# Normalisation after the product for a part of a projection, with a new order of loads

## The chip, the cores and the metric

The kernel runs on one core of a Trainium2 chip. The metric is the device time of one execution in microseconds. Matrix products run on TensorE (PE in the profile), elementwise work on VectorE (DVE) and ScalarE (ACT), transfers are issued by SyncE (SP) and by ScalarE.

## The reference

One layer works on a residual stream `x` of 512 tokens by 2048 features. What matters here is its beginning:

```python
mod = c_act @ w_ada[l] + b_ada[l]
shift, scale, gate = jnp.split(mod, 3, axis=-1)
h = rms_norm(x) * (1.0 + scale[:, None, :]) + shift[:, None, :]
proj = h @ w_in[l]
xr, gr, qc, kvc, kr, ga = jnp.split(proj, split_points(IN_SPLITS), axis=-1)
```

`rms_norm` multiplies each token by the reciprocal root of its mean square. `proj` has 4160 columns. Then come a recurrent branch (convolution, gates, scan), a latent attention with eight heads, both with gates, and an output product with 2048 x 2048 weights. All is float32.

## The kernel before

Features lie on the partitions and tokens run along the 512 columns of a tile. The features are cut into 16 blocks of 128 (index k). The wide projection's columns are cut into 32 output tiles of 128 (index m, in the order `MORDER`) and a narrow one of 64 for `kr`. Every float32 factor is split into a high and a low part, so that a product of one block with one output tile is three matmuls of 512 columns: high weight by high `h`, high weight by low `h`, low weight by high `h`. For weights, ScalarE copies the raw tile to `whi` and VectorE subtracts to get `wlo` (`wload`, L193); two buffers of each stand in the first phase, and three to five raw ones.

**The start.** SP's queue carries first the eight half rows of `xtok` (512 KB each), whose squares are summed by ScalarE and VectorE (`xsq`, L364), then `vec`, `m0` (the scale columns for block 0, 1 MB) and pieces of the modulation matrix. From the sums comes `rx`, the factor per token (L411 to L418). The heads of `xtok` are multiplied by `rx`, transposed on TensorE (L436), and scaled to block 0 of `h`. The scale column for block 0 is a product of 16 small matmuls into `mr_ps`, copied to a row and turned into a column by `m0_ps`. `junk` matmuls (`warm`) fill TensorE at three places. Block 0 of the first eight output tiles is multiplied by exact float32 products (`wfraw`), two passes each.

**Rows.** Each shift or scale column of the other blocks is a row sum: 1 MB of `ada` is loaded, multiplied by the broadcast `cb` and summed by one VectorE instruction (`ttr`, L271). A scale row and a shift row make one `h` block (`make_h`, L453): two VectorE passes and one of ScalarE. Three buffers hold rows.

**Chunks.** The 16 blocks are multiplied in four chunks (`CHUNKS`: 2, 3, 4 and 7 blocks). Within a chunk the output tiles go by groups (`proj_group`, L522); after each chunk a tile's sum is copied (first chunk, ScalarE) or added (VectorE) to its slot `pj` (`evac`, L512). The rows for the next chunk are spread over the groups of this one (L579 to L584). The last chunk (7 blocks, `proj_last`) runs together with the recurrent branch, then attention and the output product follow.

**Order.** SP's order is that of the program text. The other engines' orders are laid out by the scheduler of the framework, from a simulated timeline; `tc.issue_after` puts an instruction behind a given one. `setup_rope` (rotary tables) and `setup_sp` (constants of the recurrence) stand in the last chunk (`SETUP`, L740 to L743).

Of the kernel before, what the change touches and what calls it, by code (L numbers as in the profile page):

```python
# [12 lines left out]
F32 = mybir.dt.float32  # L13
# [7 lines left out]
P = 128  # L21
# [4 lines left out]
CHUNKS = ((0, 2), (2, 3), (5, 4), (9, 7))  # L26
# [6 lines left out]
NF = 8  # L33
GROUP = (4, 2, 2, 1)
AHEAD = (0, 1, 0)
# [5 lines left out]
SETUP = (0, 2)  # L41
WARM = (4, 5, 2)
SQ_V = (3, 6)
# [40 lines left out]
def body(ctx, nc, tc, a):  # L84
# [49 lines left out]
    def mm_hi(out, wh, c0, xs, start):  # L134
        for i, (xh, xl) in enumerate(xs):
            mm(out, wh[:, cols(c0 + i)], xh, start and i == 0, False)
            mm(out, wh[:, cols(c0 + i)], xl, False, False)

    def mm_lo(out, wl, c0, xs, stop):
        for i, (xh, _) in enumerate(xs):  # L140
            mm(out, wl[:, cols(c0 + i)], xh, False, stop and i == len(xs) - 1)
# [51 lines left out]
    def wload(src, n):  # L193
        raw = wraw()
        DMA.dma_start(out=raw[:, :n], in_=src)
        hi, lo = wtile("whi", "whi"), wtile("wlo", "wlo")
        wlast[0] = ins_of(split(hi[:, :n], lo[:, :n], raw[:, :n]))
        return hi, lo
# [12 lines left out]
    ktab = pjt(33, F32, "ktab").rearrange("p (f i c) -> p f i c", f=2, i=NT)  # L211
# [5 lines left out]
    c4 = pjt(20, F32, "c4")[0:4]  # L217
    A.dma_start(out=c4, in_=a["c"])
    ccol = p1.tile([P, NK], F32, name="ccol")
    A.dma_start(out=ccol, in_=a["ccol"])  # L220
    id4 = p1.tile([4, 4], F32, name="id4")
    A.dma_start(out=id4, in_=a["row"][0:4, R_ID:R_ID + 4])
# [9 lines left out]
    ch, cl = (pjt(21 + i, F32R, f"c4{n}")[0:4] for i, n in enumerate("hl"))  # L232
    sel = pjt(23, F32R, "sel")[0:4].rearrange("p (q o) -> p q o", q=4)
    V.tensor_copy(out=sel, in_=id4.rearrange("p (q o) -> p q o", o=1).broadcast_to([4, 4, P]))
    tab(c4, c4, AF.Silu)
    V.tensor_copy(out=ch, in_=c4)
    tt(cl, c4, ch.bitcast(F32), ALU.subtract)

    junk = p1.tile([P, S], BF16, name="junk")
    V.memset(junk, 1.0)  # L240
    junk_ps = bank("aux", "junk_ps")

    def warm(n, after=None):
        with tc.issue_after(ins_of(after)) if after is not None else nullcontext():
            for _ in range(n):
                mm(junk_ps, junk[:, :P], junk, True, True)

    warm(WARM[0])
    cps = [bank("mm", "cb_ps") for _ in range(4)]
    for r in (ch, cl):  # L250
        for q in range(4):
            mm(cps[q], sel[:, q], r, r is ch, r is cl)
    for q in range(4):
        V.tensor_copy(out=cb[:, q], in_=cps[q])
# [4 lines left out]
    def xslot(name):  # L259
        n = xn[0]  # L260
        xn[0] += 1
        return pjt((36, 37, 34, 35)[n % 4], F32, name)
# [15 lines left out]
    def ada(j, parts=(4,)):  # L278
        t = p1.tile([P, 4, S], F32, tag="ada", name="ada", bufs=3)
        n0 = 0  # L280
        for w in parts:
            c = slice(n0, n0 + w)
            DMA.dma_start(out=t[:, c], in_=a["ada"][j][:, n0 * S:(n0 + w) * S].rearrange("p (k s) -> p k s", k=w))
            ttr(t[:, c], cb[:, c], j, n0 == 0, n0 + w == 4)
            n0 += w
            yield


    def setup_rope():
        rt = [pjt(34 + i, F32, f"rt{i}") for i in range(2)]  # L290
# [49 lines left out]
    def setup_sp():  # L340
# [3 lines left out]
        act(ab, lam, AF.Abs)  # L344
# [17 lines left out]
    sqj, sqv = (bigt(n, "sqj").rearrange("p k s -> p (k s)") for n in (15, 14))  # L362

    def xsq(i, j):  # L364
        t = bigt((2, 3, 8, 9, 10, 11, 12, 13)[2 * i + j], "xtok").rearrange("p k s -> p (k s)")
        DMA.dma_start(out=t, in_=a["xtok"][i][:, j * 1024:(j + 1) * 1024])
        s = ss8[:, j * 4 + i:j * 4 + i + 1]
        if 2 * i + j in SQ_V:
            sq = V.tensor_tensor_reduce(out=sqv, in0=t, in1=t, op0=ALU.mult, op1=ALU.add, scale=1.0, scalar=0.0,
                                        accum_out=s)  # L370
        else:
            sq = act(sqj, t, AF.Square, accum_out=s)
        if not i and not j:
            with tc.issue_after(ins_of(sq)):
                tab(ccol, ccol, AF.Silu)
        if j == 0:
            xhead.append(t[:, :KT0 * P])
        warm(WARM[1], sq)

    hh, hl, xhead = {}, {}, []  # L380
    KT0 = CHUNKS[0][1]
    NG = NF // 4
    wfs = {(k, n): bigt(4 + k * NG + n, "wfs", F32R) for k in range(1, KT0) for n in range(NG)}
    wfraw = {kn: pjt(16 + i, F32, "wfraw") for i, kn in enumerate((k, n) for k in range(KT0) for n in range(NG))}

    def wf_load(k, n):
        raw = wfraw[k, n]
        DMA.dma_start(out=raw, in_=a["winf"][k, n])
        if k:
            act(wfs[k, n][:, 0], raw, AF.Copy)  # L390

    def wf_lo(k, n):
        tt(wfs[k, n][:, 1], wfraw[k, n], wfs[k, n][:, 0].bitcast(F32), ALU.subtract)

    A.dma_start(out=ident, in_=a["row"][:, R_ID:R_ID + P])
    xps = [bank("mm", "xps") for k in range(KT0)]
    for n in range(2 * NT):
        xsq(n // 2, n % 2)
    DMA.dma_start(out=vec, in_=a["vec"])
    ts(vec[:, 16:32], vec[:, 16:32], 1.0, None, ALU.add)  # L400

    m0 = [bigt(4 + q, "m0").rearrange("p k s -> p (k s)").rearrange("p (b f) -> p b f", b=8) for q in range(2)]
    for q in range(2):
        DMA.dma_start(out=m0[q], in_=a["ada0"][:, 8 * q:8 * q + 8])
    run(ada(0, (2, 2)))
    for n in range(NG):
        wf_load(0, n)
    tab(p1.tile([P, 1], F32, name="sqrt0"), ones[:, 0:1], AF.Sqrt)


    vx, yx, tx, rx = (p1.tile([P, NT], F32, name=n) for n in ("vx", "yx", "tx", "rx"))  # L411
    tt(vx, ss8[:, 0:4], ss8[:, 4:8], ALU.add)
    ts(vx, vx, 1.0 / D, EPS, ALU.mult, ALU.add)
    V.reciprocal(out=tx, in_=vx)
    tab(yx, tx, AF.Sqrt)
    tt(tx, yx, yx, ALU.mult)
    stt(tx, tx, -0.5, vx, ALU.mult, ALU.mult)
    mark[0] = ins_of(stt(rx, tx, 1.5, yx, ALU.add, ALU.mult))  # L418

    for i in range(NT):  # L420
        if i % 2:
            ts(xhead[i], xhead[i], rx[:, i:i + 1], None, ALU.mult)
        else:
            act(xhead[i], xhead[i], AF.Copy, scale=rx[:, i:i + 1])

    mr_ps, m0_ps = bank("mm", "mr_ps"), bank("mm", "m0_ps")
    rb_ps = bank("aux", "rb_ps")

    for b in range(NK):
        i = mm(mr_ps[0:1, 0:P], ccol[:, b:b + 1], m0[b // 8][:, b % 8], b == 0, b == NK - 1)  # L430
    mrow = pjt(24, F32, "mrow")[0:1, 0:P]
    act(mrow, mr_ps[0:1, 0:P], AF.Copy)
    with tc.issue_after(ins_of(i)):
        for k in range(KT0):
            for i in range(NT):
                t = PE.transpose(xps[k][:, cols(i)], xhead[i][:, cols(k)], ident)  # L436
    with tc.issue_after(ins_of(t)):
        i = mm(m0_ps[:, 0:1], mrow, ones[0:1, 0:1], True, True)
    tt(mod[:, 16:17], m0_ps[:, 0:1], vec[:, 16:17], ALU.add)
    with tc.issue_after(ins_of(i)):  # L440
        for i in range(NT):
            t = mm(rb_ps[:, cols(i)], rx[:, i:i + 1].broadcast_to([P, P]), ident, True, True)
    warm(WARM[2], t)
    xt[0] = xps[0]
    for k in range(1, KT0):
        xt[k] = pjt(34 + k, F32, f"x{k}")
        act(xt[k], xps[k], AF.Copy)
    rb = p1.tile([P, S], F32, tag="rb", name="rb")
    act(rb, rb_ps, AF.Copy)

    h0 = []

    def make_h(k):  # L453
        if 0 < k < KT0:
            yield from ada(16 + k, (2, 2))
            yield from ada(k, (2, 2))
        x, sc, sh = xt[k], mod[:, 16 + k:17 + k], mod[:, k:k + 1]
        t = bigt(k, f"h{k}", F32R)
        hh[k], hl[k] = t[:, 0], t[:, 1]
        if k < KT0:  # L460
            xs = pjt(30 + k, F32, "xs")
            if k == 0:
                h0.append(xs)
                mark[0] = ins_of(ts(xs, x, sc, sh, ALU.mult, ALU.add))
                split(hh[k], hl[k], xs)
            else:
                act(xs, x, AF.Copy, scale=sc)
                ts(hh[k], xs, sh, None, ALU.add)
                mark[0] = ins_of(stt(hl[k], xs, sh, hh[k].bitcast(F32), ALU.add, ALU.subtract))
        else:  # L470
            stt(x, x, sc, rb, ALU.mult, ALU.mult)
            act(hh[k], x, AF.Identity, bias=sh)
            stt(hl[k], x, sh, hh[k].bitcast(F32), ALU.add, ALU.subtract)
        if not k:
            yield

    rows = [f + k for k in range(KT0, NK) for f in (16, 0)]
    tiles, loaded, summed = [], [0], [0]  # L480

    def row_load():
        j = rows[loaded[0]]
# [758 lines left out]
```

## Time and profile before

| | |
|---|---|
| time, median of three runs | 714.48 us (714.46 to 715.6) |
| span of the profiled execution | 712.3 us |
| TensorE busy | 706.0 us, 99% |
| VectorE busy | 537.5 us, 75% |
| ScalarE busy | 356.5 us, 50% |
| first projection matmul starts | 22.47 us |
| matmuls and weight loads | 3284 each |
| bytes moved | 131.60 MB, mean 185 GB/s |

The page names lines of the kernel (L124 is the helper that issues a matmul), an operation's output and inputs by tile names, and for groups the busy time and the mean duration of one. The time between instructions of one engine is put down to what released the next. The granted clock of TensorE is 1.00 nearly throughout.

### The profile page before, as it was taken

What the parts mean: (1) busy time and instruction counts of PE and PEld (TensorE: products, weight loads), DVE (VectorE), ACT (ScalarE), POOL (GpSimd) and SP (SyncE); (2) the same over time, 40 slices, a digit from 0 to 9 for tenths busy, and PEclk for the clock granted to TensorE, in tenths of its full rate; (3) what the DMA queues carried; (4) which work ended last, traced back from release to release, by engine and by line L of the source; (5) the groups of instructions that cost most, each with busy time, mean ns of one, the idle gap of its engine ahead of it and who ended that gap; (6) DMA issues with size and microseconds to landing.
All of it is one profiled execution on the core that took longest, in us unless ns stands there. A gap on an engine that the chain in (4) does not pass through costs nothing.

```text
span 712.3 us, 9598 instructions
## 1 busy us (share of the span) xinstructions
PE 706.0 (99%) x3284; PEld 579.7 (81%) x3284; DVE 537.5 (75%) x1008; ACT 356.5 (50%) x767; POOL 33.3 (5%) x50
## 2 busy tenths in 40 slices
PE   8999999999999999999999999999999999999997
PEld 4688888888888888888888898888888888788886
DVE  4857999899997989888756666659797886683332
ACT  6376222222223589885455677687766433222220
POOL 0000000000000000001002102002110000000000
PEclk9999999999999999999999999999999999999999
DMA  9998777697532422233253326323552887875320
GB/s 337 408 399 315 262 278 265 248 343 293 197 140 75 137 82 79 77 91 104 70 163 108 107 86 208 111 74 117 157 184 82 301 271 271 282 253 175 117 88 30
DMA packets 48880, 131.60 MB, mean 185 GB/s; under 512 B 5820, under 2 KB 12860, under 8 KB 45248
## 3 DMA queue, kind: packets, MB, share of 16 engines
q1 hardware_dynamic: 41472, 109.94, 44.9%
q10 hardware_dynamic: 7360, 21.06, 8.4%
q8 instruction: 26, 0.43, 0.2%
q14 instruction: 22, 0.18, 0.1%
HBM read 126.78 MB, written 4.19 MB: 184 GB/s over the span
## 4 chain that ended last, share of the span: by engine, by line
PE 95%; DMA 3%; DVE 1%; issue 0%; SPq 0%; ACT 0%; ACTq 0%; DVEq 0%
PE pp L124 48%; PE oa L124 24%; PE uwkv L124 6%; PE uwq L124 5%; PE sc L124 4%; PE op L124 2%; DMA ada<-in_ada 1%; PE tp L945 1%; DMA xtok<-in_xtok 1%; PE pk L124 1%; PE tq L857 1%; PE pi L124 1%; PE pr L124 1%; DMA ccol<-in_ccol 1%; DVE ada L273 1%; PE tqe L905 0%
## 5 line engine op out<-in xcount | busy, mean ns | idle before, releaser
L124 PE MATMUL pp<-h,whi 128*128 128x512 f32 x992 | 240.8, 390 | 0.0
L89 ACT ACTIVATE whi<-wraw 128x512 fp32r<-128x512 f32 (+4 forms) x192 | 136.5, 717 | 196.8 <-PE pp L124 100.3
L124 PEld LDWEIGHTS pp<-h,whi 128*128 128x128 f32 x992 | 185.7, 188 | 38.6 <-ACT whi L89 0.2
L117 DVE TENSOR_TENSOR wlo<-wraw,whi 128x512 fp32r<-128x512 f32 (+4 forms) x192 | 150.9, 791 | 69.7 <-ACT whi L89 34.5
L124 PE MATMUL pp<-h,wlo 128*128 128x512 f32 x496 | 126.9, 390 | 0.0
L124 PEld LDWEIGHTS pp<-h,wlo 128*128 128x128 f32 x496 | 92.9, 188 | 19.0
L124 PE MATMUL oa<-yl,whi 128*128 128x512 f32 (+1 forms) x260 | 100.9, 389 | 0.0
L124 PE MATMUL oa<-yh,whi 128*128 128x512 f32 (+1 forms) x260 | 100.1, 390 | 0.1
L117 DVE TENSOR_TENSOR pj<-pp,pj 128x512 f32<-128x512 f32 x96 | 64.7, 685 | 15.1 <-PE pp L124 14.8
L124 PE MATMUL oa<-yh,wlo 128*128 128x512 f32 (+1 forms) x260 | 71.0, 390 | 0.0
L273 DVE CUSTOM_DVE_ANT_0 ada<-ada,cb,vec 128x2048 f32<-128x2048 f32 (+1 forms) x31 | 69.5, 2242 | 1.7 <-DMA ada<-in_ada 1.7
L124 PEld LDWEIGHTS oa<-yh,whi 128*128 128x128 f32 x260 | 48.7, 188 | 10.2 <-ACT yh L89 0.5
L124 PEld LDWEIGHTS oa<-yl,whi 128*128 128x128 f32 x260 | 48.9, 188 | 9.3
L124 PEld LDWEIGHTS oa<-yh,wlo 128*128 128x128 f32 x260 | 47.8, 188 | 9.4
L124 PE MATMUL uwkv<-whi,kvt 128*128 128x512 f32 x80 | 28.4, 398 | 0.0
L228 POOL TENSOR_TENSOR hs<-hs,mhalf 128x4 f32<-128x4 f32 (+1 forms) x20 | 24.5, 1227 | 1.6
L124 PE MATMUL uwq<-whi,kvt 128*128 128x384 f32 x80 | 24.1, 344 | 0.1
L89 ACT ACTIVATE PT<-tp 128x128 f32<-128x128 f32 (+3 forms) x32 | 14.0, 438 | 19.1 <-PE tp L945 10.8
L124 PE MATMUL sc<-kT,qT 128*128 128x128 f32 (+3 forms) x96 | 23.0, 327 | 0.0
L273 DVE CUSTOM_DVE_ANT_0 ada<-ada,cbo,vec 128x1024 f32<-128x1024 f32 x16 | 20.4, 1278 | 3.1 <-DMA ada<-in_ada 3.1
L273 DVE CUSTOM_DVE_ANT_0 ada<-ada,cbo,modh 128x1024 f32<-128x1024 f32 x16 | 20.5, 1279 | 1.9 <-DMA ada<-in_ada 1.9
L101 DVE SCALAR_TENSOR_TENSOR xo<-oa,mod,xo 128x512 f32<-128x512 f32 (+1 forms) x12 | 8.2, 704 | 17.6 <-PE oa L124 17.6
(215 smaller groups left out, 888.9 us busy)
## 6 DMA issues: line engine op xcount, KB each, us to landing
ada<-in_ada SPq DMA_DIRECT2D x28, 1024.0 KB, 5.9
ada<-in_ada ACTq DMA_DIRECT2D x32, 512.0 KB, 5.2
wraw<-in_wout SPq DMA_DIRECT2D x59, 256.0 KB, 3.8
wraw<-in_win SPq DMA_DIRECT2D x22, 512.0 KB, 5.7
wraw<-in_win SPq DMA_DIRECT2D x24, 448.0 KB, 3.2
wraw<-in_win SPq DMA_DIRECT2D x16, 384.0 KB, 5.3
wraw<-in_wkv SPq DMA_DIRECT2D x24, 256.0 KB, 3.2
wraw<-in_wq SPq DMA_DIRECT2D x24, 192.0 KB, 2.5
```

The source lines that it names most:

```text
L89: return A.activation(out=out, in_=in_, func=func, **kw)
L101: return V.scalar_tensor_tensor(out=out, in0=in0, scalar=scalar, in1=in1, op0=op0, op1=op1, **kw)
L117: return V.tensor_tensor(out=o, in0=x, in1=y, op=op)
L124: return PE.matmul(out=out, lhsT=lhsT, rhs=rhs, start=start, stop=stop, **kw)
L228: G.tensor_tensor(out=out, in0=out, in1=mhalf[:, :n], op=ALU.pow)
L273: ttr_last[0] = V.tensor_tensor_reduce(out=t, in0=t, in1=cv, op0=ALU.mult, op1=ALU.add, scale=1.0, scalar=vec[:, C_BADA + j:C_BADA + j + 1 ...
L857: PE.transpose(tp[:, d * 256 + i2 * P:d * 256 + (i2 + 1) * P], kt[:, q * P:(q + 1) * P], ident)
L945: PE.transpose(tp[:, j * P:(j + 1) * P], pr[:, j * P:(j + 1) * P], ident)
```

## The change

The factor per token is the same for all blocks of features, so it can be applied to a sum. For the first `N1` = 18 output tiles and the first `KE` = 4 blocks, the product is made with `e = x * (1 + scale)`, without the factor and without the shift. These sums wait in their slots. When the tile's next chunk (blocks 4 to 8) comes, VectorE writes slot times `rb` (the factor, spread over the partitions) into the PSUM bank, and the matmuls add to it. The shift's part is a constant per output column: `b0`, a row product of the weights (`w0t`, the same weights once more, transposed, 4.5 MB) with the shift, added in the last chunk.

The other 14 output tiles take blocks 0 to 8 in one chunk with the full `h`. So there are chunks of 4 and 5 blocks, or of 9, and one of 7. The first eight tiles of each kind run as a stream, block by block, in eight banks, with weights of 4 output tiles (256 KB) at a time. Weight loads are fetched up to three ahead (`wnext`).

The order of loads is new: `m0`, `x0` and `wu` come first in SP's queue, `ccol`, `c4i` and `vec` are on ACT's; then come the scale rows 17 to 19; the squares of `xtok` follow between the streams' loads, all on ScalarE, and `root` makes `rx` and `rb` afterwards. Block 0 comes from `x` itself, without the transposes. The full `h` of blocks 0 to 3 is made later. `setup_sp` and `setup_rope` move from the last chunk into the second. Four products of block 0 are exact float32 ones instead of eight. The junk matmuls are 8 and 3 instead of 28, 16 and 2.

The core of the diff:

```diff
-CHUNKS = ((0, 2), (2, 3), (5, 4), (9, 7))
+KE, KM = 4, 9
+KRS = ((0, 4), (4, 5), (9, 7))
-NF = 8
-GROUP = (4, 2, 2, 1)
-AHEAD = (0, 1, 0)
+NS = 8
+N1 = 18
+DEPTH = 3
+PACE = 15
+GROUP = (4, 2, 1, 1)
+RS2 = {0: 10, 1: 11, 2: 12, 3: 13, 4: 15, 5: 16, 6: 17, 7: 18, 8: 19}
-SETUP = (0, 2)
-WARM = (4, 5, 2)
-SQ_V = (3, 6)
+SETUP = (2, 6)
+WARM = (8, 3)
...
+    A.dma_start(out=c4i, in_=a["c4i"])
+    A.dma_start(out=vec, in_=a["vec"])
...
+    def xsq(n):
+        i, j = n // 2, n % 2
+        t = bigt((4, 5, 7, 8, 13, 14)[n % 6], "xtok").rearrange("p k s -> p (k s)")
         DMA.dma_start(out=t, in_=a["xtok"][i][:, j * 1024:(j + 1) * 1024])
...
+    for q in range(2):
+        DMA.dma_start(out=m0[:, 8 * q:8 * q + 8], in_=a["ada0"][:, 8 * q:8 * q + 8])
+    xload(0)
+    DMA.dma_start(out=wu, in_=a["winu"])
...
+    x0b = x0t[:, 0]
+    act(x0b, xt[0], AF.Copy, scale=vec[:, 16:17])
+    warm(WARM[0])
...
     for b in range(NK):
+        if b == NK // 2:
+            spread(ch)
+        chain(lambda: mm(mr_ps[0:1, 0:P], ccol[:, b:b + 1], m0[:, b], b == 0, b == NK - 1))
+    mrow = pjt(12, F32, "mrow")[0:1, 0:P]
+    V.tensor_copy(out=mrow, in_=mr_ps[0:1, 0:P])
+    spread(cl, range(2))
+    chain(lambda: mm(m0_ps[:, 0:1], mrow, ones[0:1, 0:1], True, True))
+    spread(cl, range(2, 4))
+    warm(WARM[1])
+    xs0 = xst[:, 0]
+    mark[0] = ins_of(stt(xs0, xt[0], m0_ps[:, 0:1], x0b, ALU.mult, ALU.add))
...
+    rows = [16 + k for k in range(1, KE)] + list(range(KE)) + [f + k for k in range(KE, NK) for f in (16, 0)]
...
+            mark[0] = wlast[0] if tie is None else tie
+            if summed[0] == 3:
+                mark[0] = rxi[0]
...
+            if 16 < j < 16 + KE:
+                k = j - 16
+                early(k)
+                act(eh[k][0], xt[k], AF.Copy, scale=mod[:, j:j + 1])
+                stt(eh[k][1], xt[k], mod[:, j:j + 1], eh[k][0].bitcast(F32), ALU.mult, ALU.subtract)
+            elif j < 16:
+                make_h(j)
...
+    def preload(m, p):
+        tt(p, slot[m], rb, ALU.mult)
...
+    def group(ms, xparts, again=False):
         ps = [bank("mm", "pp") for _ in ms]
+        if again:
+            for m, p in zip(ms, ps):
+                preload(m, p)
...
     def proj_last(n, kind, parts):
...
+                if n < N1:
+                    stt(slot[m], ps, b0[:, n:n + 1], slot[m], ALU.add, ALU.add)
+                else:
+                    tt(slot[m], ps, slot[m], ALU.add)
...
+    def bias(n):
+        t = bigt(n % 3, "w0t")
+        DMA.dma_start(out=t, in_=a["w0t"][n].rearrange("p (k s) -> p k s", k=2))
+        with tc.issue_after(wlast[0]):
+            for i in range(2):
+                V.tensor_tensor_reduce(out=t[:, i], in0=t[:, i], in1=shrow, op0=ALU.mult, op1=ALU.add,
+                                       scale=1.0, scalar=0.0, accum_out=b0[:, 2 * n + i:2 * n + i + 1])
...
+    def ahead1(k, tie):
+        row_sums(min(k + 1, 3), tie)
+        if k:
+            squares(k)
+
+    stream(MORDER[:NS], range(KE), eh, ahead1)
...
+    es = [eh[k] for k in range(KE)]
+    ng = (N1 - NS) // 2
+    for g in range(ng):
+        group(MORDER[NS + 2 * g:NS + 2 * g + 2], [es])
+        squares(3 + 3 * (g + 1))
+        if nsq[0] == 8:
+            row_sums(3 + 2 * (g - 1))
+
+    def ahead2(k, tie):
+        row_sums(RS2[k], tie)
+
+    stream(MORDER[N1:N1 + NS], range(KM), late(), ahead2)
+    n0 = summed[0]
+    NB1 = 32 - N1 - NS
+    steps = [(MORDER[n:n + 1], False) for n in range(N1 + NS, 32)] + [(MORDER[n:n + 1], True) for n in range(N1)]
+    for g, (ms, again) in enumerate(steps):
+        if g == SETUP[0]:
+            with tc.issue_after(wlast[0]):
+                setup_sp()
+        if g == SETUP[1]:
+            with tc.issue_after(wlast[0]):
+                setup_rope()
+        at = 9 * min(g + 1, NB1) + 5 * max(0, g + 1 - NB1)
+        row_sums(min(len(rows), n0 + (len(rows) - n0) * at // (9 * NB1 + 5 * N1 - PACE)))
+        if again:
+            group(ms, [hs(KE, KM)], True)
+        else:
+            group(ms, [hs(0, KE), hs(KE, KM)])
...
+        if g == NB1:
+            ps, shrow = bank("mm", "sh_ps"), bigt(3, "shrow")[:, 0]
+            for i in range(KE):
+                spread_col(ps, i, mod[:, i:i + 1])
+            act(shrow, ps, AF.Copy)
...
+        if g >= NB1 and (g - NB1) % 2 == 0:
+            bias((g - NB1) // 2)
```

The prediction calls the work on the first 18 output tiles with blocks 0 to 3 the first stream (eight tiles) and the groups (ten tiles), the next eight tiles with blocks 0 to 8 the second stream, the six tiles after them the six outputs, and the return to the 18 tiles with blocks 4 to 8 the second block.

398 lines of the change are left out of this document (183 added, 215 removed).

## The prediction

> **What bounds the kernel now.** I began with the page, whose busy times say that TensorE works through almost the whole span.
>
> ```profile
> span 712.3 us, 9598 instructions
> PE 706.0 (99%) x3284; PEld 579.7 (81%) x3284; DVE 537.5 (75%) x1008; ACT 356.5 (50%) x767; POOL 33.3 (5%) x50
> ```
>
> The median of the runs is 714.48 us, so 2.2 us lie around the span; the sums below are made in the span and get 2.2 us at the end. Does this busy time hide waits? The chain of waits in order of time (start, length, what) has a long piece of projection matmuls, and the table by stretches (length, busy time and count of PE, PEld, DVE, ACT, POOL, granted clock, DMA share, GB/s) shows VectorE beside it:
>
> ```profile
> 103.15 76.16 PE pp L124 x336
> ...
> 100.00:120.00 20.00, 20.00 (x90) 16.54 (x90) 19.40 (x25) 6.43 (x8) 0.00 (x0) 1.00 0.75 277
> 140.00:160.00 20.00, 20.00 (x90) 16.57 (x89) 20.00 (x24) 5.20 (x6) 0.00 (x0) 1.00 0.79 301
> ```
>
> 76.16/336 is 0.2267 us per 128x512 matmul, with VectorE at 97 to 100% and TensorE not waiting. So TensorE bounds everything after its first projection matmul, and two things can move the time: when that matmul starts, and whether VectorE or a transfer ever comes late. The start is in the timeline:
>
> ```profile
> 1.59 8.34 PE L124 MATMUL junk_ps<-junk 128*128 128x512 bf16 x28 [1.59 <-DVE spe L350]
> 4.75 1.06 ACT L89 ACTIVATE sqj<-xtok 128x1024 f32<-128x1024 f32 x1 [0.74 <-DMA xtok<-in_xtok]
> 5.41 0.15 PEld L124 LDWEIGHTS <-junk 128*128 128x128 bf16 x1 [0.28 <-issue]
> 5.83 3.60 PEld L124 LDWEIGHTS <-junk 128*128 128x128 bf16 x17 [0.28 <-issue]
> 6.21 0.22 ACT L89 ACTIVATE ccol<-ccol 128x16 f32<-128x16 f32 x1 [0.31 <-DMA ccol<-in_ccol]
> 9.86 1.19 PE L124 MATMUL cb_ps<-c4h,sel 4*128 4x512 f32 x4
> 14.64 1.06 ACT L89 ACTIVATE sqj<-xtok 128x1024 f32<-128x1024 f32 x1 [1.44 <-DMA xtok<-in_xtok]
> 16.13 3.65 PE L124 MATMUL mr_ps<-m,ccol 128*1 128x128 f32 x32 [0.61 <-DVE vx L117]
> 19.82 0.27 ACT L89 ACTIVATE mrow<-mr_ps 1x128 f32<-1x128 f32 x1 [1.65 <-PE mr_ps L124]
> 20.74 0.38 PE L124 MATMUL m_ps<-ones,mrow 1*128 1x1 f32 x2
> 21.05 1.16 PE L124 MATMUL rb_ps<-row,rx 128*128 128x128 f32 x8
> 21.38 0.81 DVE L114 TENSOR_SCALAR xs<-xps,mod 128x512 f32<-128x512 f32 x1
> 22.47 7.03 PE L124 MATMUL pp<-xs,wfraw 128*128 128x512 f32 x16
> 29.82 5.72 PE L124 MATMUL pp<-h,wfs 128*128 128x512 f32 x24 [0.32 <-DVE h L113]
> ```
>
> ScalarE's squares begin when a piece of `xtok` lands: the first at 4.75, the eighth at 14.64. That is (14.64 - 4.75)/7 = 1.41 us for each 512 KB once the queue runs. The scale block comes behind all eight, and the first projection matmul starts at 22.47.
>
> **The start, part by part.** The change sends the scale block `m0` (two units of 512 KB) first, then `x0` and `wu` (half a unit each). By the pitch above, unit n lands at 4.75 + 1.41(n - 1): `m0` at 4.75 and 6.2, `x0` at 6.9, `wu` at 7.6. `ccol` is now ACT's first transfer. The 32 dot-product instructions (3.65/32 = 0.114 each) run in two halves of 1.83. Junk matmuls were spaced 0.42 (5.41 to 5.83) and then 3.60/17 = 0.21, so until 5.83 I count double: the first half runs from 4.75 to 7.1. Between the halves stand four `cb_ps` matmuls (1.19), whose `c4i` is ACT's second transfer; `ccol`, second before, was read at 6.21, so silu, cast and split are done near 7.3. Second half: 8.5 to 10.3. Then the row copy (0.27), the one-column matmul (0.38) and the scaling of `x0` (like L114, 0.81), with 0.05 to 0.15 from one to the next: 11.95. The before needs 22.47 - (21.38 + 0.81) = 0.28 from there to the matmul. So it starts at **12.2 instead of 22.47: -10.3 us**. Bounds: 11.4 if `c4i` lands as early as `m0`; 16.5 if TensorE stays at the slow pace (1.8 more in each half, 0.6 in the spread).
>
> The granted clock reads 1.00 in every stretch, while those junk matmuls halve their spacing at 5.83, so that column doesn't show the pace here. [...]
>
> **TensorE's content.** Before: 7.35 us from 22.47 to 29.82 for eight exact fp32 products in two passes each. After: four, 7.03/2 = 3.51, and the twelve split matmuls that take the place of the other four, 12 x 0.2267 = 2.72. The spread of `rx` (1.16) was ahead of the first product and is now inside the stream; the spread of the four shift columns adds another 1.16. The projection is otherwise the same in count; `proj_kr` has two matmuls for each block in three chunks as in four. Net **+1.2 us**.
>
> **What lies beside it.** The durations (busy, mean ns | idle before):
>
> ```profile
> L273 DVE CUSTOM_DVE_ANT_0 ada<-ada,cb,vec 128x2048 f32<-128x2048 f32 x28 | 65.7, 2345 | 0.7 <-DMA ada<-in_ada 0.7
> L117 DVE TENSOR_TENSOR pj<-pp,pj 128x512 f32<-128x512 f32 x96 | 64.7, 685 | 15.1 <-PE pp L124 14.8
> L117 DVE TENSOR_TENSOR wlo<-wraw,whi 128x512 fp32r<-128x512 f32 x92 | 62.9, 687 | 45.2 <-PE oa L124 20.5 <-ACT whi L89 19.1 <-PE pp L124 2.3
> L117 DVE TENSOR_TENSOR wlo<-wraw,whi 128x1024 fp32r<-128x1024 f32 x22 | 26.7, 1215 | 7.5 <-ACT whi L89 7.5
> L117 DVE TENSOR_TENSOR wlo<-wraw,whi 128x768 fp32r<-128x768 f32 x16 | 15.2, 949 | 4.4 <-ACT pj L89 4.4
> L273 DVE CUSTOM_DVE_ANT_0 ada<-ada,cbo,modh 128x1024 f32<-128x1024 f32 x16 | 20.5, 1279 | 1.9 <-DMA ada<-in_ada 1.9
> L101 DVE SCALAR_TENSOR_TENSOR x<-x,mod,rb 128x512 f32<-128x512 f32 x14 | 10.4, 745 | 0.1
> ```
>
> On a full queue the instructions overlap a little, so a start-to-start price is lower:
>
> ```profile
> 102.62 2.34 DVE L273 CUSTOM_DVE_ANT_0 ada<-ada,cb,vec 128x2048 f32<-128x2048 f32 x1
> 104.89 0.08 DVE L273 DVE_READ_ACCUMULATOR2_ANT mod<- 128x1 f32 x1
> 104.89 0.68 DVE L117 TENSOR_TENSOR pj<-pp,pj 128x512 f32<-128x512 f32 x1
> 105.50 0.68 DVE L117 TENSOR_TENSOR pj<-pk,pj 128x512 f32<-128x512 f32 x1
> 106.09 0.95 DVE L117 TENSOR_TENSOR wlo<-wraw,whi 128x768 fp32r<-128x768 f32 x1
> 106.96 0.74 DVE L101 SCALAR_TENSOR_TENSOR h<-x,mod,h 128x512 fp32r<-128x512 f32 x1
> 107.62 1.28 DVE L117 TENSOR_TENSOR pj<-pp,pj 128x512 f32<-128x512 f32 x2
> ```
>
> A row sum takes 2.27, an evacuation 0.60, an `h` half 0.66, and a split 0.09 less than its duration. The rotary setup, tile `rt` alone, summed over four stretches from 160 to 240 us:
>
> ```profile
> sum 80.00, DVE 9.54 ACT 0.51; mean DVE 2.39 ACT 0.13
> ```
>
> No row shows a split of 640 columns (0.82 between 512 and 768; 0.73 on a full queue), a 512-column row product (half of 1279 plus a start: 0.75; 0.67) or an addition that writes PSUM (`preload`; 0.685 from the evacuation that reads it; 0.60).
>
> *First stream* (12.2 to 34.7). Scale row 17 is complete with unit 7, at 13.2. VectorE must first write `cb` and the low half of `e0` (about 2 us from 11.95), then sum the row and make `e1`: 17.1 to 17.9. TensorE has 3.51 + 2.72 us of block 0 and asks for `e1` at 18.4. Rows 18 and 19 land at unit 10.5 (18.1) and 15 (24.5), are ready near 21.8 and 28.2, and are asked for at 23.8 and 29.3. Margins of 0.5 to 2 us; I charge 0.5.
>
> *Groups and second stream* (34.7 to 111). The squares end with unit 26, near 40; `rx` can follow well before TensorE reaches block 0 of the second stream at 62. From 40 to 62 VectorE has three 1024-splits (3.4), six row sums (13.6) and five `h` (6.6): 23.6 for 22 us. The second stream asks 18 x 0.60 + 10 x 2.27 + 5 x 1.32 = 40 of 49 us. Tiles are now 12 matmuls (2.7 us) long instead of 18, with two buffers; a row sum ahead of a split still fits into the 2.7 + 1.8 us until its low half is wanted. Nothing charged, bound 3.7 (the same 22 us at full durations, 25.7).
>
> *Second block* (18 outputs of 15 matmuls, 61.2 + 1.16 = 62.4 us). VectorE: 18 x (0.73 + 0.60) + 18 x 0.67 + 7 x 2.27 + 4 x 1.32 + 9.54 = 66.8, so 4.4 us too much; at full durations 74.5, so 12.1. The last three outputs carry no row sum, the six outputs before (36.7 us for 27 us of VectorE) leave room for a lead of one tile, and the products for `b0` may slip into the last phase, which no longer has the rotary setup. I charge 2.0 of the 4.4. Below nothing no stage can go, since the pace is TensorE's own.
>
> The last phase exchanges an addition for one with a scalar (0.685 to 0.745), hidden under 21 matmuls of 0.2267; 4.5 MB of `w0t` and the second pass over x spread over the second block (18.5 MB in 62 us, about 300 GB/s against rates above 400 in the start). ScalarE, at 50%, takes 18 evacuations more.
>
> **Sum.** 712.3 - 10.3 + 1.2 + 0.5 + 2.0 = 705.7; with 2.2: **707.9, say 708 us**.
>
> **Rivals.**
> A, the forecast: 705.5 to 711.
> B, all VectorE work fits: 708 - 2.5 = 705.5, down to 704.5 with the early start. For it: stretches at 100% without a wait.
> C, slower: VectorE bounds the second block. Its place is the queue between row sums, rotary setup and the splits that TensorE waits for; it decides once the lead of one tile (15 matmuls, 3.4 us) is used up. Full durations instead of overlapped ones, and the overhang of the groups: 703.2 + 12.1 + 3.7 + 2.2 = 721 us; half of it is 713. For it: the sum of 66.8 against 62.4. Against it: the full stretches above.
> D, the slow pace until the stream: start at 16.5, 4.3 later: 712.
> E, the scale rows come late. The rates in the start decide:
>
> ```profile
> 10.00:15.00 5.00, 5.00 (x23) 2.71 (x24) 4.05 (x9) 2.81 (x7) 0.00 (x0) 1.00 1.02 413
> 25.00:30.00 5.00, 4.68 (x12) 1.92 (x11) 4.57 (x8) 1.98 (x3) 0.00 (x0) 1.00 1.06 412
> ```
>
> My pitch of 1.41 us for each 512 KB is 372 GB/s, below these 412, but part of it is the wait for the queue's first piece, and a load on ACT's queue shares it. If each of the three rows lands 1 us past its margin, 708 + 3 = 711. [...]
> F, the change doesn't do what it says: `m0` first but `c4i` or `vec`, both on ACT's queue, gate the chain near 22. Against it: the rows at 6.21 show a small ACT load landing within 5 us beside a full queue. Then nothing is won at the start: 712.3 + 1.2 + 2.5 + 2.2 = 718.
>
> **How the numbers follow.** A 0.50, B 0.14, D 0.10, E 0.10, C 0.13, F 0.03. From no change 0.2% (1.4 us: 713.1 to 715.9) can be told. C up to half its price and the high ends of D and E reach into that band (0.07 together); the rest of C and F lie above it: faster 0.81, same 0.07, slower 0.12. The range takes A, B, D, E and the low part of C: 704 to 714.
>
> **What would show it.** First `pp` matmul at 12.2, not 16; no `pp` matmul waiting on `e1` to `e3`; the stretch of `winc` tiles with VectorE near 100% and TensorE idle no more than 2 us. Wrong if `whi`, `wlo` or a DVE write of `pp` releases TensorE for more than 5 us in sum, or if the junk spacing stays at 0.42 into the dot products.

## The result, and the profile after

The changed kernel takes **705.83 us** (median; 705.49 to 706.34), the kernel before beside it on the same chip 714.47 us (713.68 to 715.6). The ratio is **0.988, with a 95% interval of 0.9866 to 0.9894**: faster by 1.2%. The forecast was 708.0 us with a range of 704 to 714, so the sign and the range hold and the size is 2.2 us short of what came. The profiled execution took 705.81 us, with 704.0 us of span, against 712.3 us of span before: 8.3 us less.

The page's head and its line of busy times, for the changed kernel:

```profile
span 704.0 us, 9647 instructions
PE 697.4 (99%) x3252; PEld 576.4 (82%) x3253; DVE 523.3 (74%) x1010; ACT 376.0 (53%) x812; POOL 34.9 (5%) x50
```

The shares are nearly those of before. TensorE still works through the whole span, so the difference has to be sought at the places where it does not. The timeline of the changed kernel (start, length, engine, what; in brackets the idle time before it and what ended that) has the start, one row spread over the columns, and the two later places where TensorE waited:

```profile
0.71 0.41 ACTq L226 DMA_DIRECT2D ccol<-in_ccol  x1
5.21 0.21 ACT L92 ACTIVATE ccol<-ccol 128x16 f32<-128x16 f32 x1 [1.76 <-DMA ccol<-in_ccol]
5.47 1.91 PE L127 MATMUL mr_ps<-m,ccol 128*1 128x128 f32 x16 [0.29 <-ACT ccol L92]
7.31 1.21 PE L127 MATMUL cb_ps<-c4h,sel 4*128 4x512 f32 x4
8.45 1.91 PE L127 MATMUL mr_ps<-m,ccol 128*1 128x128 f32 x16
9.63 1.36 DVE L120 TENSOR_TENSOR wlo<-wraw,whi 128x512 fp32r<-128x512 f32 x2 [1.55 <-ACT whi L92]
10.91 0.27 DVE L400 COPY mrow<-mr_ps 1x128 f32<-1x128 f32 x1
...
12.78 3.60 PE L127 MATMUL pp<-xs,wu 128*128 128x512 f32 x8
...
15.81 2.41 PE L127 MATMUL pp<-e,whi 128*128 128x512 f32 x8
17.34 0.75 DVE L104 SCALAR_TENSOR_TENSOR e<-x,mod,e 128x512 fp32r<-128x512 f32 x1 [0.79 <-ACT e L92]
18.97 1.98 PE L127 MATMUL pp<-e,whi 128*128 128x512 f32 x8
...
52.74 1.05 PE L127 MATMUL rb_ps<-row,rx 128*128 128x128 f32 x8
53.55 1.64 PE L127 MATMUL pp<-e,whi 128*128 128x512 f32 x6
...
135.50 0.77 PEld L127 LDWEIGHTS pp<-h,wlo 128*128 128x128 f32 x4 [0.47 <-DVE wlo L120]
...
214.52 0.49 DVE L120 TENSOR_TENSOR ktab<-rt,row 128x128 f32<-128x128 f32 x2
215.10 0.72 ACT L92 ACTIVATE h<-x,mod 128x512 fp32r<-128x512 f32 x1 [1.61 <-DVE ktab L120]
215.73 0.58 ACT L92 ACTIVATE pj<-pp 128x512 f32<-128x512 f32 x1
216.36 3.49 PE L127 MATMUL pp<-h,whi 128*128 128x512 f32 x14 [0.51 <-ACT pj L92]
```

The first projection matmul starts at 12.78 instead of 22.47: **9.7 us earlier**. From there to the end of the span the kernel before took 712.3 - 22.47 = 689.8 us and this one takes 704.0 - 12.78 = 691.2: **1.4 us more**. The two make the 8.3 us.

The table by stretches (length; busy time and count of PE, PEld, DVE, ACT, POOL; granted clock, DMA share, GB/s), for the first stream, the second block and the stretch behind it:

```profile
12.00:35.00 23.00, 22.84 (x94) 17.47 (x95) 15.31 (x20) 12.70 (x22) 0.00 (x0) 1.00 1.02 399
...
148.00:214.00 66.00, 66.00 (x293) 54.67 (x292) 62.28 (x134) 28.93 (x45) 0.00 (x0) 1.00 0.79 291
214.00:330.00 116.00, 115.49 (x520) 95.51 (x519) 100.21 (x151) 84.94 (x127) 4.98 (x6) 1.00 0.31 98
```

The second row holds the second block. TensorE is busy for 66.00 of 66 us there, and VectorE for 62.28: close to full, with 3.7 us left. The groups of VectorE's instructions (mean ns behind the busy time) price the three operations that had no row before:

```profile
L120 DVE TENSOR_TENSOR wlo<-wraw,whi 128x640 fp32r<-128x640 f32 x24 | 19.7, 820 | 1.8 <-ACT whi L92 1.1 <-PE pp L127 0.6
...
L120 DVE TENSOR_TENSOR pp<-pj,rb 128x512 f32<-128x512 f32 x18 | 12.4, 694 | 0.0
...
L584 DVE CUSTOM_DVE_ANT_0 w0t<-w0t,shrow 128x512 f32<-128x512 f32 x18 | 11.7, 685 | 0.4 <-DMA w0t<-in_w0t 0.4
```

### The profile page after: what moved, and what is told of

Same layout as the page of the kernel before. It is cut to its first block, busy times and chain, and to the rows that moved or that the text cites. A ratio compares the mean times of both kernels' runs of the same rounds, so it can differ in the third digit from the quotient of the medians.

```text
span 704.0 us, 9647 instructions
## 1 busy us (share of the span) xinstructions
PE 697.4 (99%) x3252; PEld 576.4 (82%) x3253; DVE 523.3 (74%) x1010; ACT 376.0 (53%) x812; POOL 34.9 (5%) x50
## 4 chain that ended last, share of the span: by engine, by line
PE 95%; DMA 2%; DVE 1%; ACT 1%; issue 1%; SPq 0%; DVEq 0%; ACTq 0%
PE pp L127 47%; PE oa L127 25%; PE uwkv L127 6%; PE uwq L127 5%; PE sc L127 4%; PE op L127 2%; PE tp L1001 1%; DMA ada<-in_ada 1%; PE pk L127 1%; PE tq L913 1%; PE pi L127 1%; PE pr L127 1%; DMA ccol<-in_ccol 1%; DMA wraw<-in_winsa 1%; PE tqe L961 0%
## 5 line engine op out<-in xcount | busy, mean ns | idle before, releaser
L92 ACT ACTIVATE whi<-wraw 128x512 fp32r<-128x512 f32 (+4 forms) x214 | 142.3, 670 | 177.3 <-PE pp L127 72.2
L127 PE MATMUL pp<-h,whi 128*128 128x512 f32 x880 | 215.6, 390 | 0.5 <-ACT pj L92 0.5
L120 DVE TENSOR_TENSOR wlo<-wraw,whi 128x512 fp32r<-128x512 f32 (+4 forms) x214 | 156.2, 735 | 77.6 <-ACT whi L92 39.0
L127 PEld LDWEIGHTS pp<-h,whi 128*128 128x128 f32 x880 | 164.6, 188 | 34.9 <-ACT pj L92 0.9
L127 PE MATMUL pp<-h,wlo 128*128 128x512 f32 x440 | 114.8, 390 | 0.0
L127 PEld LDWEIGHTS pp<-h,wlo 128*128 128x128 f32 x440 | 82.2, 188 | 17.0 <-DVE wlo L120 0.5
L275 DVE CUSTOM_DVE_ANT_0 ada<-ada,cb,vec 128x2048 f32<-128x2048 f32 x31 | 72.7, 2348 | 3.2 <-DMA ada<-in_ada 3.2
L92 ACT ACTIVATE pj<-pp 128x512 f32<-128x512 f32 x50 | 29.4, 599 | 26.9 <-PE pp L127 26.6
L127 PE MATMUL pp<-e,whi 128*128 128x512 f32 x136 | 34.5, 393 | 0.0
L127 PEld LDWEIGHTS pp<-e,whi 128*128 128x128 f32 x136 | 25.5, 188 | 5.7 <-issue 0.5
```

What stands on the lines that cost most here:

```text
L92: return A.activation(out=out, in_=in_, func=func, **kw)
L120: return V.tensor_tensor(out=o, in0=x, in1=y, op=op)
L127: return PE.matmul(out=out, lhsT=lhsT, rhs=rhs, start=start, stop=stop, **kw)
L275: ttr_last[0] = V.tensor_tensor_reduce(out=t, in0=t, in1=cv, op0=ALU.mult, op1=ALU.add, scale=1.0, scalar=vec[:, C_BADA + j:C_BADA + j + 1 ...
```

## The experiments

Each edit below also changes the order of other instructions on the engines, since that order is worked out for the whole program. A small difference between two kernels can come from this alone (the run with the row copy first shows a wait of 0.8 us that came so), and is read from the trace rather than from the time.

### The pieces of x ahead of the scale block

The question is whether the place in the queue is what brought the 9.7 us. Six pieces of x (3 MB) are loaded ahead of `m0`, and the squares use them later as before:

```diff
+    for n in range(6):
+        xtok_load(n)
     for q in range(2):
         DMA.dma_start(out=m0[:, 8 * q:8 * q + 8], ...)
```

> Six of the eight xtok pieces (3 MB) are loaded ahead of m0 in SP's queue; their squares stay where they were in the program. Theory (the gain is the earlier first product, and that is the place of m0 in the queue): m0 lands six pitches of 1.41 us later, 8.5 us; its second half at 14.7 plus 1.9 us of dot products, and from the second half's start to the first pp matmul 4.3 us as in the changed kernel: first pp matmul near 20.6 instead of 12.8, time 705.8 + 7.8 = 713 to 714 us, back at the time of before. Rival (the gain lies in the new chunks and in VectorE's relief, the start being hidden by other work): 706 to 708.

Measured: **720.22 us** (717.42 to 722.03), ratio 1.0081 (1.0054 to 1.0108), span 718.7. The whole gain is gone and 6 us more. From its timeline and its waits (what waited for what: us in total, times, longest; the first two lines are TensorE's, the last is VectorE's from 35 to 162 us):

```profile
13.28 3.57 PE L127 MATMUL mr_ps<-m,ccol 128*1 128x128 f32 x16 [8.09 <-DMA m<-in_ada]
...
21.90 2.31 PE L127 MATMUL pp<-xs,wu 128*128 128x512 f32 x5
```

```profile
PE pp L127 <- DVE wlo L120: 2.2, 3, 1.1
PE pk L127 <- DVE wkhl L120: 1.8, 1, 1.8
...
DVE ada L275 <- DMA ada<-in_ada: 11.7, 7, 2.5
```

The dot products wait 8.1 us for `m0`, and the first half of them takes 3.57 us instead of 1.91: after the wait TensorE runs slowly. The first `pp` matmul comes at 21.90, 9.1 us later. So the order of the queue is worth the gain of the start, nearly to the microsecond. The theory had named 20.6 us for this matmul and a time of 713 to 714: the span grew by 14.7, 5.6 more than the start. By the starts of TensorE's matmuls, 5.1 us went to waits on `wlo` and `wkhl`, splits on VectorE, while the 1.1 us of waits of the changed kernel (at 135 and 215 us) are not in this run: 4.0 us net. VectorE's line of the same view, for the changed kernel, gives the reason:

```profile
DVE ada L275 <- DMA ada<-in_ada: 3.2, 4, 1.6
```

Where a row sum stood at the head of VectorE's list and its scale row had not landed, the splits behind it stood too (rows of such a place, at 117 us, are in the next run): 11.7 us of such waits instead of 3.2. The last 1.6 us stand behind the longest of TensorE's waits for a split, in the timeline and in the table by stretches:

```profile
160.00 4.15 PE L127 MATMUL pk<-h,wkhl 128*128 128x512 f32 x10 [1.84 <-DVE wkhl L120]
```

```profile
160.30:164.10 3.80, 3.80 (x11) 2.93 (x10) 2.26 (x9) 0.00 (x0) 0.00 (x0) 0.55 0.28 84
```

Eight matmuls there stand 0.427 us apart, from start to start, instead of 0.227, which makes the 1.6 us, and the granted clock is 0.55.

### The scale block first, the pieces of x ahead of the scale rows

The second half of "scale rows first": the same six loads, behind the first weight tiles and ahead of the first scale row.

```diff
     def ahead1(k, tie):
+        if not k:
+            for n in range(6):
+                xtok_load(n)
         row_sums(min(k + 1, 3), tie)
```

> The same six xtok pieces are loaded behind the first three weight pieces and ahead of x1 and the first scale row; m0 keeps its place. Theory (the margins of the scale rows are about 2 us or less, so their place in the queue carries the gain as well): row 17 lands near 21.7 instead of 13.2, e1 is ready near 25 while TensorE asks for it at 19.0; one wait of 5 to 6.5 us in the first stream, none at e2 and e3, time 711 to 712.5. Rival (the rows have slack, or the loads run faster than my pitch): 706 to 707.5.

Measured: **718.13 us** (717.18 to 718.26), ratio 1.0051 (1.0035 to 1.0068), span 716.3. From its timeline:

```profile
25.40 5.38 PE L127 MATMUL pp<-e,whi 128*128 128x512 f32 x12 [6.17 <-ACT e L92]
...
117.06 2.35 DVE L275 CUSTOM_DVE_ANT_0 ada<-ada,cb,vec 128x2048 f32<-128x2048 f32 x1 [2.98 <-DMA ada<-in_ada]
...
119.34 1.29 DVE L120 TENSOR_TENSOR wlo<-wraw,whi 128x512 fp32r<-128x512 f32 x2
120.08 0.19 PEld L127 LDWEIGHTS pp<-h,wlo 128*128 128x128 f32 x1 [2.59 <-DVE wlo L120]
```

and its first stretch in the table by stretches:

```profile
12.00:35.00 23.00, 16.67 (x55) 11.66 (x56) 12.54 (x16) 11.28 (x20) 0.00 (x0) 0.85 0.91 358
```

The start is that of the changed kernel (12.81), and the wait is where the theory put it: 6.2 us on `e1`. But it cost more than its length. The twelve matmuls behind it take 5.38 us; they stand 0.427 us apart, from start to start, instead of 0.227, so 2.5 us come on top, and the granted clock of the stretch falls to 0.85. Then late scale rows come back at 117: VectorE waits 2.98 us for one, the splits behind it start at 119.34, and TensorE stands still until 120.08. Its waits for splits sum to 2.7 us on `wlo` and 0.5 on `wkhl`, 4.4 by the starts of its matmuls. Counted up by these starts, 6.3 + 2.5 + 4.4, less the 1.1 us of the changed kernel's waits that are not in this run, is 12.1 of the 12.3 us by which the span grew. The theory had the wait right and neither of its two consequences.

Slow matmuls, 0.427 against 0.227 us, came here behind a wait of 6.2 us. A wait need not be that long, though: in the run before, one of 1.8 us was followed by eight matmuls at 0.427 us. Why that one was, and the 2.2 us wait at 120 us in this run was not, stays open.

### No junk matmuls at the start

Rival D has TensorE at the slow pace until the stream. This run takes away the eight junk matmuls ahead of the dot products.

```diff
-WARM = (8, 3)
+WARM = (0, 3)
```

> The eight junk matmuls at the start are left out; the three later ones stay. [...] Rival (the pace has become full by 5.5 us whatever ran before, or the waits in the chain swallow it): first pp matmul within 0.5 us of 12.8, time 705.5 to 706.5.

Measured: **707.09 us** (706.9 to 710.22), ratio 0.9911 (0.9888 to 0.9934), span 705.1. From its timeline:

```profile
5.36 3.29 PE L127 MATMUL mr_ps<-m,ccol 128*1 128x128 f32 x16 [5.36 <-ACT ccol L92]
...
9.70 1.91 PE L127 MATMUL mr_ps<-m,ccol 128*1 128x128 f32 x16
...
13.55 1.88 PE L127 MATMUL pp<-xs,wu 128*128 128x512 f32 x4
```

Without them the first half of the dot products takes 3.29 us, 1.38 more, and the second half runs at full pace. The first `pp` matmul comes 0.77 us later, less than the 1.38, because the changed kernel's row copy waited for VectorE anyway (below). So the slow pace is real (3.29 us for 1.91) and lasts until about 8.1 us here (an estimate: at 0.114 us for a dot product at full pace and twice that at the slow one, the 1.38 us are twelve slow ones), and the eight junk matmuls are worth 0.8 us beside this profile of the changed kernel (0.45 beside its repeat, further below, where the first `pp` matmul starts at 13.10), not the 4.3 of rival D. The rival's figures did not come: 13.55 is 0.77 us from 12.8, not within 0.5, and 707.09 lies above its 705.5 to 706.5.

### More work for VectorE in the second block

This asks how far the second block is from rival C, in which VectorE bounds it. Eighteen more row products of 512 columns go behind those for `b0`, two for each `w0t` tile; their sums go to columns that nobody reads. A second kernel has nine of them (the first of each pair).

```diff
+                V.tensor_tensor_reduce(out=t[:, i], in0=t[:, i], in1=shrow, ...,
+                                       accum_out=bx[:, i:i + 1])
```

> Each of the 18 row products for b0 is followed by one more of the same size into an unused column: 18 x 0.69 = 12.4 us more of VectorE in the second block, nothing else. Theory (VectorE is within some 4 us of bounding the second block: 62.3 us busy in the 66 us from 148 to 214): 12.4 - 3.7 = 8.7 us too much, of which the last phase may take a little: 711 to 715. Rival (single small operations fill gaps and the surplus is put off into the last phase, where nothing waits): 706 to 708.

> Nine extra row products of 512 columns on VectorE in the second block (6.2 us at 0.69 each), half of what the run with eighteen had; the output is as before, the extra sums are not used. Theory (the second block has about 4 us of slack on VectorE, the 12.4 us of eighteen products cost 8.4): 2 us, 708 (ratio 0.991), with VectorE at 65 of 66 us from 148 to 214 us. Rival (VectorE is in series with TensorE at some places of the block, each product costs its share): 4.2 us, 710 (0.9938). Second rival (slack is larger, and the cost of the eighteen sat elsewhere): 705.8.

Measured: with nine **709.16 us** (708.45 to 710.1), ratio 0.9933 (0.992 to 0.9945), span 707.0; with eighteen **714.19 us** (712.63 to 717.45), ratio 1.0002 (0.9989 to 1.0014), span 712.5. The row of the second block in the table by stretches, with nine:

```profile
148.00:214.00 66.00, 64.41 (x282) 52.35 (x281) 64.12 (x139) 27.22 (x41) 0.00 (x0) 1.00 0.77 283
```

and with eighteen, with the largest of TensorE's waits behind it:

```profile
148.00:214.00 66.00, 62.26 (x270) 49.94 (x269) 65.39 (x143) 25.67 (x40) 0.00 (x0) 1.00 0.75 282
```

```profile
PE pp L127 <- DVE wlo L120: 3.7, 3, 1.3
```

The same line with nine, and, from the timeline with eighteen, the wait at the start of the last phase:

```profile
PE pp L127 <- DVE wlo L120: 1.6, 3, 0.7
```

```profile
228.77 1.58 PE L127 MATMUL pp<-h,whi 128*128 128x512 f32 x3 [1.92 <-ACT h L92]
```

At 0.69 us each the added work is 6.2 and 12.4 us; the span grew by 3.0 and 8.5. If the 3.7 us that VectorE has free in the second block are used first, 2.5 and 8.7 are left to pay, which is the first theory of both runs. The numbers are near, but the trace does not bear the sum out. By the starts of TensorE's matmuls, the waits for splits inside the block cost 2.4 us with nine and 5.0 with eighteen, and the wait for `h15` at the start of the last phase grew by 0.6 and 1.4: together about 3.0 and 6.4. The rest of the 8.5 is 1.8 us of slow matmuls behind that last wait (0.427 us apart) and 0.4 at the start, neither of them a wait for VectorE. So half of the added work cost about half of the waits, and VectorE was still idle for 1.88 of the 66 us with nine. That the slack is larger than the 6.2 us (705.8) is refuted. That each product costs a share of itself, the rival of the run with nine, is not; its 4.2 us were half of a growth that was not all waits, and its ratio (0.9938) lies inside the measured interval, that of the theory (0.991) outside. What is shown is that the mechanism of rival C is there: TensorE waits for splits as soon as 6.2 us are added. That a slack of 3.7 us must be used up first is not shown.

### The row copy ahead of two splits

The timeline after shows the dot products done near 10.4 (8.45 + 1.91) and the row copy at 10.91: VectorE was still with two splits, taken up at 9.63 while it had nothing else. Here the first of them is put behind the scaling of `x0`.

```diff
-        return wsplit(raw, n)
+        first, early_w[0] = early_w[0], None
+        return wsplit(raw, n, first)
```

> The low half of the first weight tile is put behind the scaling of x0 on VectorE, so that the row copy no longer stands behind two splits there. Theory (of the 0.58 us that the start came later than worked out, most is VectorE's order): the row copy starts within 0.1 us of the last dot product instead of 0.55 us behind it, the first pp matmul comes about 0.5 us earlier, counted from the first dot product, and the time is 705.3 (ratio 0.9872). Rival (something else is late next, so that the copy's place is worth nothing): first pp matmul as in the changed kernel, 705.8, or later if the split that is now behind the scaling comes late for its matmuls.

Measured: 706.39 us (705.42 to 706.88), ratio 0.9891 (0.9877 to 0.9904), span 703.6. Its timeline:

```profile
10.24 0.28 DVE L400 COPY mrow<-mr_ps 1x128 f32<-1x128 f32 x1 [2.02 <-PE mr_ps L127]
...
12.14 3.60 PE L127 MATMUL pp<-xs,wu 128*128 128x512 f32 x8
...
17.98 2.35 DVE L275 CUSTOM_DVE_ANT_0 ada<-ada,cb,vec 128x2048 f32<-128x2048 f32 x1 [0.82 <-DMA ada<-in_ada]
...
20.26 0.75 DVE L104 SCALAR_TENSOR_TENSOR e<-x,mod,e 128x512 fp32r<-128x512 f32 x1
...
21.06 1.20 PE L127 MATMUL pp<-e,whi 128*128 128x512 f32 x4 [0.77 <-DVE e L104]
```

The copy comes at once and the first `pp` matmul 0.64 us earlier (0.50 counted from the first dot product, as the theory had it). But 0.8 us come back at 21 us: the low half of `e1`, at 17.34 in the changed kernel, now stands behind the second row sum and is made at 20.26. So the rival is right on the time: what was won was given back at the next operand, though not at the split that it named.

### The rotary setup earlier, and the edits together

The wait at the start of the last phase (0.51 us by the row at 216.36; by the starts of TensorE's matmuls 0.8) can be followed back in the rows of the timeline: ScalarE cannot write `h15` before the rotary setup, which has the same buffer, is done with it at 215.0; the evacuation that TensorE waits for stands behind `h15` on ScalarE. The setup starts two outputs earlier here:

```diff
-SETUP = (2, 6)
+SETUP = (2, 4)
```

> The rotary setup begins two tiles earlier (before the fifth of the six outputs, where VectorE has room). Theory (the 0.8 us stall at the start of the last phase comes from the rotary table that ends late: h15 takes its buffer, and ScalarE waits for it with an evacuation behind): the stall is gone, TensorE's matmuls run without a gap over 0.3 us from 195 to 225 us, time 705.0 (ratio 0.9867). Rival (the stall belongs to the change of phase whatever the table does, or the rotary setup now comes in the way of splits of the six outputs): a gap as long at the same place or a new one between 135 and 155 us, 705.8 or more.

> The edits of the two kernels before this one together. Theory (both waits stand on the path that sets the end, and TensorE does nothing else in them): the gains add, 704.5 (ratio 0.986). Rival (gains are taken back by later waits, since transfers and splits come no sooner): 705.3 to 706.

Measured: the rotary setup earlier takes **704.99 us** (704.43 to 706.27), ratio 0.9879 (0.9864 to 0.9894), span 702.6; with the row copy first as well 705.99 us (705.83 to 706.43), ratio 0.9888 (0.9874 to 0.9901), span 704.2. In the first one TensorE is busy for all of the stretch in which it waited before:

```profile
214.00:330.00 116.00, 116.00 (x522) 96.26 (x522) 99.43 (x146) 85.51 (x128) 4.99 (x6) 1.00 0.31 96
```

No other wait has come, and the theory holds. (The wait at 135 us is gone too, but it is also missing in the repeat of the changed kernel below, so its absence is not the edit's doing.) With both edits the wait for `e1` is back (0.7 us), as in the run before, and the gains do not add; there the rival is right.

Then the cause found for that is put to the test: both edits, and the second and third row sum put behind the low halves of `e1` and `e2`. Beside it on the same chip ran the changed kernel and the one with the earlier rotary setup, once more.

```diff
+            if 0 < summed[0] < 3:
+                mark[0] = early_lo[0]
             j = rows[summed[0]]
             ttr(tiles.pop(0), cb, j, True, True)
```

> The kernel with both edits, and in addition the second and third row sum put behind the low half of e1 and e2 on VectorE. Theory (the 0.9 us wait at 20 us that came with the earlier row copy was the low half of e1 standing behind the second row sum, and nothing else): no wait of TensorE between 12 and 140 us over 0.2 us, first pp matmul near 12.2, rotary table early, span 702.0, time 704.2. Rival (VectorE's time before the row copy was the only free place for the two splits, and their 1.3 us come back as a wait at the next place): a wait of 0.5 us or more between 18 and 35 us, span 702.6 or more.

> The changed kernel once more, beside the two others of this call on the same chip. Both theories: 705.8 (ratio 0.988), first pp matmul at 12.8 to 13.2, by the pace of the first half of the dot products (1.9 to 2.95 us in the profiles so far), and the 0.8 us wait at 215 us.

> The kernel with the earlier rotary setup once more. Theory (the 0.8 us at 215 us stand on the path that sets the end): 1.0 to 1.4 us below the changed kernel on the same chip. Rival (what is won at 215 us is in the spread of the runs, or comes back in other executions): within 0.5 us of the changed kernel.

Measured: all three edits **704.41 us** (704.05 to 704.97), ratio 0.9863 (0.9847 to 0.988), span 702.5; the earlier rotary setup alone 704.93 us (704.79 to 705.01), ratio 0.9869 (0.9854 to 0.9884), span 703.1; the changed kernel 706.22 us (705.7 to 706.57), ratio 0.9887 (0.9872 to 0.9901), span 703.8. The first stretch of the kernel with all three edits:

```profile
12.00:35.00 23.00, 23.00 (x95) 17.67 (x94) 16.52 (x22) 12.62 (x23) 0.00 (x0) 1.00 1.02 394
```

TensorE is busy for all 23.00 us, with the first `pp` matmul at 12.28, so the wait on `e1` was the low half behind the row sum and nothing else, and the two splits find another place on VectorE. The runs of this kernel lie 1.8 us below those of the changed one and do not overlap with them (the intervals of the ratios do); that is the version that **beats both kernels**. About 1.3 of the 1.8 us are the rotary setup's, which the repeat shows; the rest is near the spread of the runs, and only the trace speaks for it. The repeat of the changed kernel brought one thing that the theory had only in part:

```profile
5.28 2.90 PE L127 MATMUL mr_ps<-m,ccol 128*1 128x128 f32 x16
...
11.19 0.28 DVE L400 COPY mrow<-mr_ps 1x128 f32<-1x128 f32 x1 [0.30 <-PE mr_ps L127]
```

In this execution the first half of the dot products took 2.90 us, with the code of the one that took 1.91; the row copy is only 0.28 us later (11.19 for 10.91), since VectorE's two splits now end before the dot products do.

## Why the prediction was right, and where it was off

**What bounds the kernel.** Right: TensorE paces everything behind its first projection matmul, and the 9.7 us at the start moved the end by 9.7 less what was added behind. The run with the pieces of x ahead takes them away by one change of order.

**The sum.** The mechanism is right; that the total is only 2.2 us off is in part luck. Against the predicted terms the start cost 0.6 us more and unforeseen waits 1.1, while the content came 0.6 lower and the two charges, 0.5 and 2.0, were not called in. The 2.2 us around the span were also too many: that figure set the median of the runs against the span of one execution. Where both are known for one execution, 1.8 to 1.9 lie around the span (705.81 and 704.0 here; 714.18 and 712.3 in an execution of the kernel before).

**The start: -10.3 predicted, -9.7 measured.** The two halves of the dot products (1.91 for 1.83), the spread between them and the second half's start (8.45 for 8.5) came as worked out. What was not seen is VectorE's list: the row copy was priced with 0.05 to 0.15 us of handing over and stood 0.55 behind two splits. `ccol`, an 8 KB load, was used at 5.21, 4.5 us after its issue, and so decided the beginning of the dot products; the step had `m0` decide it, at 4.75, and counted the slow pace until 5.83, which cancelled most of that.

**TensorE's content: +1.2 predicted, +0.6 measured.** The four exact products and their successors: from 12.78 to 15.81, then 0.41 us lost ahead of the second matmul of `e0` (0.63 from the start before it to its own, in all profiles of these kernels but one), and 2.72, so 6.2 for 7.35, as predicted. A spread was charged with 1.16, the busy time of its row; it takes 0.81 until the next matmul starts (52.74 to 53.55) and 0.09 more there. Two of them are 1.8 instead of 2.3.

**First stream: 0.5 charged, 0 measured.** No matmul of `pp` waited for `e1` to `e3` here (one did, for 0.5 us at 30.5, in the run with nine more products). The estimate of the margin at `e1` was 0.5 to 2 us, and it was about 0.9 (low half ready at 18.09, first matmul of `e1` at 18.97).

**Second block: 2.0 charged, 0 measured.** This is the largest of the errors. The durations were right: 0.82, 0.69 and 0.685 for 0.82, 0.685 and 0.75. What failed first is the sentence that the six outputs "leave room for a lead of one tile". The group of the preloads over the whole span, with their first and last start, then the same group in the stretch of the block and the stretch itself (270 matmuls at 0.2267, counted back from 215.5, begin near 154):

```profile
L120 DVE TENSOR_TENSOR pp<-pj,rb x18: 690/694/697, 121.1 to 194.5; 128x512 f32<-128x512 f32 x18
```

```profile
L120 DVE TENSOR_TENSOR pp<-pj,rb 128x512 f32<-128x512 f32 x12 | 8.3, 694 | 0.0
```

```profile
153.40:215.50 62.10, 62.10 (x276) 51.40 (x274) 58.41 (x123) 26.77 (x42) 0.00 (x0) 1.00 0.81 300
```

In this kernel a preload needs only a free PSUM bank and no weights, and the kernel turns over eight banks. So six of the eighteen were made ahead of the block, the first of them 33 us ahead, and the last one 21 us before its end. The lead was counted in weight buffers and stood in PSUM banks. Six preloads (3.6 us at 0.60), one of the four pairs of passes for `h` (1.3) and 0.7 of the rotary setup lie ahead of the stretch: 5.6 of the 8.4 us from the 66.8 worked out to the 58.41 of 62.10 measured. Most of the other 2.8 is price. On the full queue a row product takes 0.61 us from start to start, not 0.67, and the rotary setup about 8 in all, not its busy time of 9.54. So part of the excess of 4.4 us over TensorE's time was never there, the lead covered the rest, and TensorE never waited inside. The run with nine products shows that this was close: with 6.2 us more, splits came late.

**What was not in the sum.** Two waits of 0.3 us (at 135) and 0.8 us (at 215), the second from the rotary setup. The prediction moved that setup from the last phase into VectorE's queue and counted its 9.5 us there; it did not ask who stands behind its last instruction, as it holds a buffer that `h15` needs. Content and waits are 0.6 + 1.1 = 1.7 for the 1.4 us measured behind the start; the 0.3 between them stays open.

**The rivals.** A had its condition only in part: the charges for the first stream and the second block were not called in, and the time lies at A's low edge. It is B's time (705.5), and B's condition holds: all VectorE work fits. C's mechanism was shown by the added products: 6.2 us more work in the second block brought 2.4 us of waits there. D cost nothing in this execution; 1.0 us of the slow pace is there in others (2.90 for 1.91), never the 3.6 that a slow pace up to the stream would take from the dot products. That the pace could stay slow so long was the author's estimate, and no run shows it. E did not come. The run with late rows shows that its price is not the sum of the lateness, row by row: one wait of 6.2 us came with 12.3 us in all, by slower matmuls behind it and splits stopped by later rows. F is refuted: `c4i` and `vec` were there before their users on TensorE's path asked.

## What to carry to other kernels

Where one engine paces the whole kernel, bringing forward its first real instruction is worth the time by which it comes earlier, less what is added behind (9.7 and 1.4 us here), and the way there was the order of the first transfers. What stands behind an instruction in an engine's list is part of its price: here a row sum that waited 2.98 us for a load held up the splits behind it, for which TensorE waited 2.2 us, and a setup without hurry held a buffer that `h15` needed, for 0.8 us of TensorE's time. Before a stage is called too full, count the lead of each of its operations by what that operation needs (a PSUM bank, a weight buffer, a row), not one lead for all.

## What the runs showed of the hardware

A wait of TensorE can cost more than its length: behind 6.2 us of waiting, twelve matmuls stood 0.427 us apart instead of 0.227, another 2.5 us. Waits of 1.8 us (pieces of x ahead, granted clock 0.55 from 160.3 to 164.1 us) and 1.9 us (eighteen more products, 0.99 over the stretch from 214 to 330) were each followed by 1.6 to 1.8 us of such loss, one of 2.2 us (scale rows late, at 120 us) by none.

Where they did not wait for `m0`, the first sixteen dot products took from 1.91 to 2.95 us in different profiles (the latter in the run with eighteen more products), with the same eight junk matmuls ahead of them, and 3.29 with none; the second sixteen took 1.91 in each. One code gave both: 1.91 and 2.90 us in two profiles of the changed kernel.

An 8 KB load (`ccol`) issued at 0.71 us on ACT's queue was used at 5.21, beside 512 KB pieces (`m0`) that were issued on SP's queue from 0.72 us on: it took 4.5 us from issue to landing, they took 4.3 and 5.1.
